# Projections of queries, keys and values with weight blocks of 512 columns, replaced in place chunk by chunk

## The chip, the cores and the metric

The kernel runs on one core of one Trainium2 chip. The metric is device time in microseconds (us) of one execution. The names of the engines are those of the profile: PE is TensorE's matmul, PEld its weight load, DVE is VectorE, ACT is ScalarE, POOL is GpSimd, SP is SyncE, which here only issues DMAs. SBUF is the on-chip memory of 128 partitions, PSUM the accumulators of the matmuls (8 banks of 512 float32 columns).

## The reference, cut to what matters

Two layers work on x of 2048 tokens by 1024. Each normalises x, multiplies it by one input matrix of 1024 by 4096, runs two attentions on the parts of the product, gates them, multiplies by an output matrix of 1024 by 1024 and adds the result to x.

```
for layer in range(DEPTH):                               # DEPTH = 2
    h = _rmsnorm(x, norm_g[layer])
    proj = jnp.einsum('bsd,dc->bsc', h, w_in[layer])     # 1024 -> 4096 columns
    qa, ka, va, ga, qd, kd, vd, gd = jnp.split(proj, cuts, axis=-1)   # 4 x 256, then 4 x 768
    oa = _stick_breaking(qa, ka, va) * silu(ga)
    qd = _partial_rope(_rmsnorm(heads(qd, 12), q_norm_g[layer]), pos)
    kd = _partial_rope(_rmsnorm(heads(kd, 12), k_norm_g[layer]), pos)
    od = _dilated_mixture(qd, kd, heads(vd, 12)) * silu(gd)
    x = x + concatenate([oa, od]) @ w_out[layer]
```

The change concerns the line `proj`, and of its 4096 columns those of qa, ka, va, qd, kd and vd (3072). The columns of ga and gd are the gates.

## The kernel before, in words

A layer has five stages: projection, stick-breaking attention (`_stick`), dilated attention (`_dilated`), output (`_output`), and then the next layer's projection. The class `Project` holds the first. Every float32 operand of a matmul is split into a high part that fp32r can hold and a low rest, and each product is three matmuls: high by high, high by low, low by high.

**The stationary and the moving operand.** `prep` (line 238) normalises 128 tokens, transposes them on PE (line 258) and stores their high and low parts, called hT. For queries, keys and values, `token_mm` (line 286) takes a 128 by 128 piece of hT as the stationary operand and 256 columns of weights as the moving one: 8 chunks k of the 1024 inputs, three matmuls each (lines 289 to 291), so 24 matmuls for 128 tokens. For the gates it is the other way round (lines 315 to 317): 128 columns of weights are stationary and 512 tokens of hT move. The output stage (lines 876, 879, 880) moves 512 columns of w_out past 128 stationary tokens.

**The weight blocks.** The loop over `cols` (line 299) goes through 16 blocks of 256 columns: three called sb (qa, ka, va), six called qk (128 columns of qd and 128 of kd each), three called v, four called g. `load_w` (line 200) loads the next block while this one is used: two DMAs or four into the raw pages H6 and H7, an ACT copy that makes the high part (line 212), and a subtraction for the low one (line 213), on POOL, except for the very first block, where it is on DVE. Blocks alternate between the pages F12, F13 and F2, F3.

**What follows a block's matmuls.** One group is 512 tokens in two PSUM banks (of four: 5, 0, 1, 2). For sb and v, DVE and ACT copy the banks to the pages S0 and S1 (lines 337 and 335), and SP stores them, for v three times in three orders (lines 346, 347, 350). For qk, ACT squares (line 356), DVE sums (line 357), POOL takes the power -0.5 (lines 135, 138), DVE scales (line 361), POOL applies gain and rotary (lines 368, 376 to 379), ACT and DVE split (lines 384, 385), PE transposes (line 393, 16 per group), DVE and ACT evict (lines 398, 396) and SP stores 512 KB at a time (line 399).

**What sets the order.** The kernel states instructions and tiles; a scheduler with a cost model of its own then fixes the order in which they stand on each engine, and places the waits. A page (F12, H6, S0, ...) is one buffer: a new tile on it waits until the last reader of the old one is done. Each engine works through its list in order, and so does SP with its DMAs.

Of the kernel before, what the change touches and what calls it, by code (L numbers as in the profile page):

```python
# [10 lines left out]
F32 = mybir.dt.float32  # L11
# [9 lines left out]
NT = 16  # L21
# [167 lines left out]
class Project:  # L189
# [10 lines left out]
    def load_w(self, parts, first=False):  # L200
# [3 lines left out]
        wh = mem.get(a, [128, NK, 256], F32R)  # L204
        wl = mem.get(b, [128, NK, 256], F32R)
# [9 lines left out]
        return wh, wl  # L215

# [5 lines left out]
    def begin(self):  # L222
# [10 lines left out]
        self.wblk = self.load_w([(0, QA, 256)], self.layer == 0)  # L233

    def hT(self, q, s, k):
        return self.hq[q][2 * s + k // 4][:, k % 4]
# [28 lines left out]
    def run(self, sb_scr, v_scr, qk_scr, g_scr, inject):  # L265
# [12 lines left out]
        r1 = xa[:, 512:768].rearrange("p (a b c) -> p a b c", a=4, c=16)  # L278
        r2 = xa[:, 768:1024].rearrange("p (a b c) -> p a b c", a=4, c=16)
# [6 lines left out]
        def token_mm(ps, wh, wl, c):  # L286
            q, cs = c // 4, slice(128 * (c % 4), 128 * (c % 4) + 128)
            for k in range(NK):
                nc.tensor.matmul(ps, hT(q, 0, k)[:, cs], wh[:, k], start=k == 0, stop=False)  # L289
                nc.tensor.matmul(ps, hT(q, 0, k)[:, cs], wl[:, k], start=False, stop=False)  # L290
                nc.tensor.matmul(ps, hT(q, 1, k)[:, cs], wh[:, k], start=False, stop=k == NK - 1)  # L291

        nxt = self.wblk
        cols = [("sb", 0, [(0, QA, 256)]), ("sb", 1, [(0, KA, 256)]), ("sb", 2, [(0, VA, 256)])]
        cols += [("qk", p, [(0, QD + 128 * p, 128), (128, KD + 128 * p, 128)]) for p in range(NPAIR)]
        cols += [("v", i, [(0, VD + 256 * i, 256)]) for i in range(3)]
        cols += [("g", 0, [(0, GA, 256)])]
        cols += [("g", 2 + 2 * i, [(0, GD + 256 * i, 256)]) for i in range(3)]
        for bi, (kind, idx, parts) in enumerate(cols):
            wh, wl = nxt  # L300
            if bi + 1 < len(cols):
                nxt = self.load_w(cols[bi + 1][2])
            if kind == "g":
                order = [(ct, tq) for ct in range(2) for tq in (2, 0, 3, 1)]
                if bi == len(cols) - 1:
                    order = [(ct, tq) for tq in (2, 0, 3, 1) for ct in range(2)]
                for gi, (ct, tq) in enumerate(order):
                    if bi == len(cols) - 1:
                        for f in inject.get(gi, ()):
                            f()  # L310
                    t = slice(512 * tq, 512 * tq + 512)
                    w = slice(128 * ct, 128 * ct + 128)
                    ps = pm.get([128, 512])
                    for k in range(NK):
                        nc.tensor.matmul(ps, wh[:, k, w], hT(tq, 0, k), start=k == 0, stop=False)  # L315
                        nc.tensor.matmul(ps, wh[:, k, w], hT(tq, 1, k), start=False, stop=False)  # L316
                        nc.tensor.matmul(ps, wl[:, k, w], hT(tq, 0, k), start=False, stop=k == NK - 1)  # L317
                    g = stg.get([128, 512])
                    nc.scalar.activation(g, ps, AF.Sigmoid)
                    nc.vector.tensor_tensor(out=g, in0=ps, in1=g, op=ALU.mult)  # L320
                    nc.sync.dma_start(out=g_scr[idx + ct, :, t], in_=g)
                continue
            for c4 in range(NT // 4):
                pss = []
                for c2 in range(2):
                    ps = pm.get([128, 2, 256])
                    for j in range(2):
                        token_mm(ps[:, j], wh, wl, 4 * c4 + 2 * c2 + j)
                    pss.append(ps)
                if kind in ("sb", "v"):  # L330
                    for c2, ps in enumerate(pss):
                        c = 4 * c4 + 2 * c2
                        st = stg.get([128, 2, 256])
                        if c2:
                            nc.scalar.copy(st, ps)
                        else:
                            nc.vector.tensor_copy(st, ps)  # L337
                        if kind == "sb":
                            nc.sync.dma_start(
                                out=sb_scr[idx].rearrange("(a c) d -> a c d", c=NT)[:, c:c + 2],  # L340
                                in_=st)
                            continue
                        for j in range(2):
                            src = st[:, j]
                            r, cc = (c + j) // 4, (c + j) % 4
                            nc.sync.dma_start(out=v_scr[idx, 0, 128 * (c + j):128 * (c + j) + 128], in_=src)
                            nc.sync.dma_start(
# [7 lines left out]
                for c2, ps in enumerate(pss):  # L355
                    nc.scalar.activation(qn[:, 2 * c2:2 * c2 + 2].rearrange("p a b c -> p a (b c)"), ps, AF.Square)
# [569 lines left out]
```

## Time and profile before

| | |
|---|---|
| median of 3 runs | 3266.57 us (3261.29 to 3266.58) |
| the profiled execution | 3269.15 us, of which the span from first to last instruction is 3267.4 us |
| PE busy | 3177.5 us, 97% of the span |
| DVE, ACT, POOL busy | 49%, 47%, 40% |
| first projection (0 to 602 us, without the gates) | PE busy 591.2 of 602 us |
| second projection (1640 to 2235 us, without the gates) | PE busy 594.3 of 595 us |
| granted TensorE clock, mean | 0.992 of full speed |

The projection without the gates takes about 1190 us of the 3267. A matmul's record lasts longer than its turn, since matmuls overlap: the time that one costs in a stream is the distance from one start to the next, which is called the pitch below. A few records of matmuls are missing from the trace, so pitches are taken between two events with a known number of matmuls between them.

### The profile page before, as it was taken

To read this page: it belongs to the slowest core of one execution; us is meant where nothing else is said; L and a number is where in the kernel's file an instruction comes from. 1 tells how busy PE (TensorE), PEld (TensorE's weight loads), DVE (VectorE), ACT (ScalarE), POOL (GpSimd) and SP (SyncE) were. 2 spreads that over 40 slices of the span, in tenths; PEclk is the share of its full clock that TensorE was granted. 3 is DMA by queue.
4 is the path that set the end of the run, shared out by engine and by line. 5 is a ranking of instruction groups with operands and counts; after the bars stand their busy time and mean duration, and the time that the engine had idled before them with its cause. 6 is when DMAs were issued, how large, how long until landed. Compare 5 with 4: busy or idle time off the path is not lost.

```text
span 3267.4 us, 66732 instructions
## 1 busy us (share of the span) xinstructions
PE 3177.5 (97%) x25808; PEld 2880.8 (88%) x25808; DVE 1605.1 (49%) x4067; ACT 1521.4 (47%) x4277; POOL 1317.2 (40%) x1342
## 2 busy tenths in 40 slices
PE   8999999999999999989999999999999999999899
PEld 8999999987777999877899999998877779988787
DVE  5034430014988777775140334301159887767721
ACT  5023221114777999962031232201147789988510
POOL 3067771012664344451021677611026744444500
PEclk9999999999999999999999999999999999999999
DMA  5222236416123556454441222363170235563443
GB/s 188 70 81 106 103 121 181 122 62 193 28 82 92 152 160 183 126 162 144 131 134 66 85 104 104 131 182 111 52 203 14 82 98 159 165 183 113 135 146 107
DMA packets 306429, 396.86 MB, mean 121 GB/s; under 512 B 16832, under 2 KB 225728, under 8 KB 295872
## 3 DMA queue, kind: packets, MB, share of 16 engines
q1 hardware_dynamic: 306112, 392.59, 39.2%
q8 instruction: 204, 3.34, 0.4%
q14 instruction: 113, 0.93, 0.1%
HBM read 235.24 MB, written 148.90 MB: 118 GB/s over the span
## 4 chain that ended last, share of the span: by engine, by line
PE 82%; DVE 5%; ACT 4%; POOL 4%; issue 3%; DMA 2%; SPq 0%; POOLq 0%; DVEq 0%; ACTq 0%
PE b L290 11%; PE b L291 11%; PE b L289 11%; PE b L676 7%; PE b L711 5%; PE b L697 5%; PE b L315 4%; PE b L317 4%; PE b L316 4%; PE b L879 3%; PE b L880 3%; PE b L876 3%; PE b L528 2%; PE b L393 2%; DVE G L495 2%
## 5 line engine op out<-in xcount | busy, mean ns | idle before, releaser
L291 PE MATMUL b<-F,F 128*128 128x256 f32 x2304 | 651.8, 283 | 0.0
L682 ACT ACTIVATE H<-H,T 128x256 f32<-128x256 f32 (+1 forms) x1152 | 522.7, 457 | 46.0 <-DVE T L678 43.7
L678 DVE CUSTOM_DVE_ANT_0 H<-b,M 128x256 f32<-128x256 f32 (+1 forms) x1152 | 368.2, 360 | 168.8 <-PE b L676 62.7
L291 PEld LDWEIGHTS b<-F,F 128*128 128x128 f32 x2304 | 440.4, 191 | 0.0
L290 PE MATMUL b<-F,F 128*128 128x256 f32 x1536 | 436.3, 284 | 0.0
L289 PE MATMUL b<-F,F 128*128 128x256 f32 x1536 | 434.9, 283 | 0.0
L290 PE MATMUL b<-F,G 128*128 128x256 f32 x1536 | 434.0, 283 | 0.0
L289 PE MATMUL b<-F,G 128*128 128x256 f32 x1536 | 433.5, 282 | 0.0
L501 POOL TENSOR_TENSOR G<-G,G 128x512 f32<-128x512 f32 (+3 forms) x320 | 320.3, 1015 | 228.9 <-DVE G L495 176.4
L676 PE MATMUL b<-F,F 128*128 128x256 f32 x2304 | 412.0, 303 | 0.3
L213 POOL TENSOR_TENSOR F<-H,F 128x1024 fp32r<-128x1024 f32 x62 | 154.2, 2500 | 605.3 <-ACT F L212 570.1
L495 DVE TENSOR_TENSOR_SCAN G<-G,b 128x513 f32<-128x513 f32 (+3 forms) x320 | 336.0, 1083 | 33.4 <-ACT G L494 33.1
L676 PEld LDWEIGHTS b<-F,F 128*128 128x128 f32 x2304 | 326.3, 190 | 20.1 <-issue 19.5
L697 PE MATMUL b<-ident,H 128*128 128x128 f32 x1800 | 293.0, 274 | 11.0 <-ACT H L699 5.5
L289 PEld LDWEIGHTS b<-F,F 128*128 128x128 f32 x1536 | 294.7, 192 | 0.0
L290 PEld LDWEIGHTS b<-F,F 128*128 128x128 f32 x1536 | 294.7, 192 | 0.0
L289 PEld LDWEIGHTS b<-F,G 128*128 128x128 f32 x1536 | 294.6, 192 | 0.0
L290 PEld LDWEIGHTS b<-F,G 128*128 128x128 f32 x1536 | 291.6, 190 | 0.0
L711 PE MATMUL b<-H,H 128*64 128x128 f32 x3600 | 229.5, 277 | 0.8 <-DVE H L699 0.8
L697 PEld LDWEIGHTS b<-ident,H 128*128 128x128 f32 x1800 | 215.5, 141 | 16.1 <-ACT H L699 8.5
L493 ACT ACTIVATE G<-b 128x512 f32<-128x512 f32 (+3 forms) x320 | 180.4, 566 | 103.5 <-PE b L486 88.3
L337 DVE COPY S<-b 128x512 f32<-128x512 f32 x48 | 33.2, 691 | 390.5 <-PE b L291 347.9
(161 smaller groups left out, 6849.0 us busy)
## 6 DMA issues: line engine op xcount, KB each, us to landing
qk_l<-H SPq DMA_DIRECT2D x96, 512.0 KB
F<-qk_l SPq DMA_DIRECT2D x48, 1024.0 KB
v_l<-S SPq DMA_DIRECT2D x288, 128.0 KB
H<-v_l SPq DMA_DIRECT2D x72, 512.0 KB
F<-qk_l SPq DMA_DIRECT2D x48, 512.0 KB
H<-in_w_in SPq DMA_DIRECT2D x40, 512.0 KB
g_l<-S SPq DMA_DIRECT2D x64, 256.0 KB
G<-mixa_l SPq DMA_DIRECT2D x32, 448.0 KB
```

What stands on the lines that cost most here:

```text
L213: (nc.vector if first else nc.gpsimd).tensor_tensor(out=wl[:, ks], in0=raw, in1=wh[:, ks].bitcast(F32), op=ALU.subtract)
L289: nc.tensor.matmul(ps, hT(q, 0, k)[:, cs], wh[:, k], start=k == 0, stop=False)
L290: nc.tensor.matmul(ps, hT(q, 0, k)[:, cs], wl[:, k], start=False, stop=False)
L291: nc.tensor.matmul(ps, hT(q, 1, k)[:, cs], wh[:, k], start=False, stop=k == NK - 1)
L493: nc.scalar.activation(g[:, 512 - n:512], z[:, :n], AF.Sigmoid, scale=-0.125)
L495: nc.vector.tensor_tensor_scan(out=r[:, 0:n + 1][:, ::-1], data0=g[:, 512 - n:513][:, ::-1], data1=z[:, 0:1].to_broadcast([128, n + 1]), i ...
L501: nc.gpsimd.tensor_tensor(out=b[:, :n], in0=b[:, :n], in1=r[:, 1:n + 1], op=ALU.mult)
L676: pin(nc.tensor.matmul(sc[:, h], qb, kv, start=s == 0, stop=s == 1))
L678: nc.vector.tensor_tensor_reduce(out=pe[:, h, :un], in0=sc[:, h, u0:u0 + un], in1=mk[:, m0:m0 + un], scale=-0.125, scalar=3.0e38, op0=ALU. ...
L682: nc.scalar.activation(pe[:, h, :un], pe[:, h, :un], AF.Exp, scale=-1.0, bias=st[:, 0, p, h, b:b + 1], accum_out=st[:, 1, p, h, b:b + 1])
L697: pin(nc.tensor.transpose(tp[:, ch, h], pe[:, h, 128 * w:128 * w + 128], ident))
L711: pin(nc.tensor.matmul(ob[64 * h:64 * h + 64, b % 4], vq[(pr * 3 + p) * 2 + (b - ch) // 8][:, (b - ch) % 8, 64 * h:64 * h + 64], ts[:, ch, h],
```

## The change: what it does

Of the twelve blocks of queries, keys and values, ten become five of 512 columns (called wide): qa with ka, three of 256 columns of qd and 256 of kd, and the first 512 of vd. The columns of va and the last 256 of vd stay blocks of 256 (narrow), va now first. The gates are as before. A wide block fills all four pages: chunks 0 to 3 of k in F2 (high) and F3 (low), chunks 4 to 7 in F12 and F13. There is no second set, so the next block's chunk is written over the old one as soon as the last group of tokens has used it. To this end the first and the last group of a block run with k as the outer loop, over two PSUM banks; the groups between run token by token. A group is now 256 tokens by 512 columns. Each chunk has a DMA of its own or two (`wide_raw`), an ACT copy and a subtraction on DVE (`wide_split`). The qk groups are stored 256 KB at a time, and the sb and v stores are as large as each row block of 256 columns.

```
     def load_w(self, parts, first=False):
-        wh = mem.get(a, [128, NK, 256], F32R)
-        wl = mem.get(b, [128, NK, 256], F32R)
+        wh, wl = (self.wt[p].rearrange("p (k f) -> p k f", k=NK) for p in (a, b))
...
+    def wide(self, k):
+        a, b = ("F2", "F3") if k < 4 else ("F12", "F13")
+        cs = slice(512 * (k % 4), 512 * (k % 4) + 512)
+        return self.wt[a][:, cs], self.wt[b][:, cs]
+
+    def wide_raw(self, parts, k):
+        if k % 2 == 0:
+            self.rawp = mem.get(f"H{6 + k // 2 % 2}", [128, 2, 512])
+        raw = self.raws[k] = self.rawp[:, k % 2]
+        for dst, col, n in parts:
+            nc.sync.dma_start(out=raw[:, dst:dst + n], in_=self.w_l[:, k, col:col + n])
+
+    def wide_split(self, k):
+        wh, wl = self.wide(k)
+        raw = self.raws.pop(k)
+        nc.scalar.copy(wh, raw)
+        nc.vector.tensor_tensor(out=wl, in0=raw, in1=wh.bitcast(F32), op=ALU.subtract)
...
-        self.wblk = self.load_w([(0, QA, 256)], self.layer == 0)
+        self.wt = {p: mem.get(p, [128, 2048], F32R) for p in ("F12", "F13")}
+        self.wblk = self.load_w([(0, VA, 256)], self.layer == 0)
...
+        def mm3(ps, c, k, wh, wl):
+            q, cs = c // 4, slice(128 * (c % 4), 128 * (c % 4) + 128)
+            nc.tensor.matmul(ps, hT(q, 0, k)[:, cs], wh, start=k == 0, stop=False)
+            nc.tensor.matmul(ps, hT(q, 0, k)[:, cs], wl, start=False, stop=False)
+            nc.tensor.matmul(ps, hT(q, 1, k)[:, cs], wh, start=False, stop=k == NK - 1)
...
+        for k in range(4):
+            self.wide_raw(wide[0][2], k)
+            self.wide_split(k)
+        narrow("sb", 2, *self.wblk, True)        # va; then raw and split of chunks 4 to 7
+        for bi, (kind, idx, parts) in enumerate(wide):
+            nxt = wide[bi + 1][2] if bi + 1 < len(wide) else None
+            for g in range(NT // 2):
+                pss = [pm.get([128, 512]) for _ in range(2)]
+                edge = g in (0, NT // 2 - 1)
+                if g == NT // 2 - 1 and nxt:
+                    for k in range(4):
+                        self.wide_raw(nxt, k)
+                for k in range(NK) if edge else (None,):
+                    for j in range(2):
+                        for kk in range(NK) if k is None else (k,):
+                            mm3(pss[j], 2 * g + j, kk, *self.wide(kk))
+                    if g == NT // 2 - 1:
+                        if nxt:
+                            self.wide_split(k)
+                            if k < 4:
+                                self.wide_raw(nxt, k + 4)
+                        elif k == 3:
+                            self.wn = 1
+                            self.wblk = self.load_w(tail[0][2])
+                if kind == "qk":
+                    qk_out(idx, pss, 2 * g)
...
+        for bi, (kind, idx, parts) in enumerate(tail):   # the last of vd, then the gates
```

On PE, before: in layer 0 the second group of the qk blocks' first one (names: output bank, then moving weights, then stationary hT), 256 columns at a time and one token block after the other.

```order
L289 MATMUL b2_201_2369<-F2_140_1439,F10_75_492 128x256
L290 MATMUL b2_201_2369<-F3_141_1440,F10_75_492 128x256
L291 MATMUL b2_201_2369<-F2_140_1439,F5_77_494 128x256
L289 MATMUL b2_201_2369<-F2_140_1439,F10_75_492 128x256
L290 MATMUL b2_201_2369<-F3_141_1440,F10_75_492 128x256
```

On PE, now: the end of the first wide qk block in layer 0 (last chunk in F12 and F13, banks 1 and 2) and the first matmul of the second one (F2, bank 5).

```order
L310 MATMUL b1_242_2248<-F13_5_213,F11_76_493 128x512
L311 MATMUL b1_242_2248<-F12_4_212,F6_78_495 128x512
L309 MATMUL b2_243_2249<-F12_4_212,F11_76_493 128x512
L310 MATMUL b2_243_2249<-F13_5_213,F11_76_493 128x512
L311 MATMUL b2_243_2249<-F12_4_212,F6_78_495 128x512
L309 MATMUL b1_242_2248<-F12_4_212,F11_76_493 128x512
L310 MATMUL b1_242_2248<-F13_5_213,F11_76_493 128x512
L311 MATMUL b1_242_2248<-F12_4_212,F6_78_495 128x512
L309 MATMUL b2_243_2249<-F12_4_212,F11_76_493 128x512
L310 MATMUL b2_243_2249<-F13_5_213,F11_76_493 128x512
L311 MATMUL b2_243_2249<-F12_4_212,F6_78_495 128x512
L309 MATMUL b5_258_2385<-F2_100_587,G1_8_222 128x512
```

A matmul now moves 512 columns, the two banks of an edge group alternate after each three matmuls, and the new block starts in the pages that the old one used first.

On POOL, before: the split of a weight block (line 213) among the qk work of layer 0.

```order
L379 TENSOR_TENSOR H2_190_2271<-X_99_585 128x16x16
L213 TENSOR_TENSOR F3_213_2468<-H6_214_2469,F2_212_2467 128x1024
L135 TENSOR_SCALAR U3_203_2419<-U3_203_2419 128x16
L213 TENSOR_TENSOR F3_213_2468<-H7_215_2474,F2_212_2467 128x1024
L138 TENSOR_TENSOR U3_203_2419<-U3_203_2419,half_67 128x16
```

On DVE, now: the splits (line 234) at the same handover as above, among the qk work of groups 5, 6 and 7 (lines 334, 338, 358, 369).

```order
L234 TENSOR_TENSOR F3_101_588<-H6_244_2250,F2_100_587 128x512 x2
L234 TENSOR_TENSOR F3_101_588<-H7_245_2255,F2_100_587 128x512
L338 TENSOR_TENSOR H2_232_2197<-b5_230_2147,U2_233_2198 128x512
L338 TENSOR_TENSOR H2_232_2197<-b0_231_2148,U2_233_2198 128x512
L234 TENSOR_TENSOR F3_101_588<-H7_245_2255,F2_100_587 128x512
L369 COPY H0_224_2117<-b3_225_2118 128x512
L234 TENSOR_TENSOR F13_5_213<-H6_246_2268,F12_4_212 128x512
L369 COPY H1_227_2132<-b6_228_2133 128x512
L234 TENSOR_TENSOR F13_5_213<-H6_246_2268,F12_4_212 128x512
L234 TENSOR_TENSOR F13_5_213<-H7_247_2289,F12_4_212 128x512
L334 TENSOR_REDUCE U3_249_2335<-H3_248_2334 128x16
L358 TENSOR_TENSOR H4_234_2212<-H2_232_2197,H4_234_2212 128x8x64
```

The subtractions have left POOL's list and stand in DVE's, half as long and twice as many, between the steps of the last groups.

On SP, now: the loads of the next block's chunks at the same handover (line 227: H6 for chunks 4 and 5, H7 for 6 and 7) and the qk stores (line 371).

```order
L371 DMA qk_l0_202<-H1_215_2031 128x2x256 x2
L227 DMA H6_246_2268<-in_w_in 128x256 x4
L227 DMA H7_247_2289<-in_w_in 128x256 x2
L371 DMA qk_l0_202<-H0_224_2117 128x2x256 x2
L371 DMA qk_l0_202<-H1_227_2132 128x2x256 x2
L227 DMA H7_247_2289<-in_w_in 128x256 x2
L227 DMA H6_344_3094<-in_w_in 128x256 x4
```

The last chunk's two loads stand behind four stores of a qk group; the raw loads for the block after next follow at once.

## Rows read from the trace of the kernel before

**Rows 1.** The page, busy time of each engine (share of the span), instructions.
```profile
PE 3177.5 (97%) x25808; PEld 2880.8 (88%) x25808; DVE 1605.1 (49%) x4067; ACT 1521.4 (47%) x4277; POOL 1317.2 (40%) x1342
```

**Rows 2.** Windows: stretch, length, busy us (instructions), granted clock, DMA share, GB/s.
```profile
190.00:480.00 290.00, 290.00 (x2535) 290.00 (x2534) 117.60 (x159) 87.02 (x146) 218.36 (x190) 1.00 0.29 102
484.00:602.00 118.00, 118.00 (x994) 118.00 (x993) 9.71 (x14) 11.97 (x18) 13.17 (x11) 1.00 0.61 178
1640.00:2235.00 595.00, 594.30 (x5091) 593.93 (x5091) 170.11 (x227) 138.64 (x233) 269.17 (x238) 1.00 0.35 116
```

**Rows 3.** The page, chain that ended last: share of the span by line.
```profile
PE b L290 11%; PE b L291 11%; PE b L289 11%; PE b L676 7%; PE b L711 5%; PE b L697 5%; PE b L315 4%; PE b L317 4%; PE b L316 4%; PE b L879 3%; PE b L880 3%; PE b L876 3%; PE b L528 2%; PE b L393 2%; DVE G L495 2%
```

**Rows 4.** Timeline, DVE in the v blocks: start, duration, line, [idle before].
```profile
524.30 0.69 DVE L337 COPY S<-b 128x512 f32<-128x512 f32 x1 [10.48 <-PE b L291]
...
570.16 0.69 DVE L337 COPY S<-b 128x512 f32<-128x512 f32 x1 [10.72 <-PE b L291]
```

**Rows 5.** Timeline, DVE in the gate blocks.
```profile
632.95 0.69 DVE L320 TENSOR_TENSOR S<-b,S 128x512 f32<-128x512 f32 x1 [4.75 <-ACT S L319]
638.39 0.69 DVE L320 TENSOR_TENSOR S<-b,S 128x512 f32<-128x512 f32 x1 [4.75 <-ACT S L319]
643.94 0.69 DVE L320 TENSOR_TENSOR S<-b,S 128x512 f32<-128x512 f32 x1 [4.86 <-ACT S L319]
...
676.78 0.69 DVE L320 TENSOR_TENSOR S<-b,S 128x512 f32<-128x512 f32 x1 [4.75 <-ACT S L319]
```

**Rows 6.** Timeline, DVE in the output stage of layer 0.
```profile
1534.21 0.69 DVE L900 TENSOR_TENSOR G<-b,G 128x512 f32<-128x512 f32 x1 [3.90 <-PE b L880]
...
1623.70 0.69 DVE L900 TENSOR_TENSOR G<-b,G 128x512 f32<-128x512 f32 x1 [3.90 <-PE b L880]
```

**Rows 7.** Groups of instructions, 190 to 480 us: busy us, mean ns, idle before.
```profile
L385 DVE TENSOR_TENSOR H<-H,H 128x512 fp32r<-128x512 f32 x46 | 34.8, 796 | 23.1 <-ACT H L384 23.1
L384 ACT CAST H<-H 128x512 fp32r<-128x512 f32 x44 | 25.1, 619 | 20.3 <-POOL H L379 20.3
L212 ACT CAST F<-H 128x1024 fp32r<-128x1024 f32 x12 | 11.9, 1046 | 0.0
L213 POOL TENSOR_TENSOR F<-H,F 128x1024 fp32r<-128x1024 f32 x12 | 31.0, 2585 | 10.4 <-ACT F L212 9.9
```

**Rows 8.** Two lines' instructions: count, duration ns min/median/max, first and last start.
```profile
L385 DVE TENSOR_TENSOR H<-H,H x96: 677/684/1550, 189.3 to 2113.0; 128x512 fp32r<-128x512 f32 x96
L213 DVE TENSOR_TENSOR F<-H,F x2: 1214/1220/1225, 10.5 to 12.2; 128x1024 fp32r<-128x1024 f32 x2
```

**Rows 9.** Timeline, 160 to 215 us, the first qk group: ACT, DVE, POOL.
```profile
176.05 0.60 ACT L356 ACTIVATE H<-b 128x512 f32<-128x512 f32 x1 [5.06 <-PE b L291]
181.21 1.29 DVE L361 TENSOR_TENSOR H<-b,U 128x512 f32<-128x512 f32 x2 [3.32 <-POOL U L138]
186.92 0.74 POOL L379 TENSOR_TENSOR H<-X 128x256 f32<-128x256 f32 x1
189.33 1.28 DVE L385 TENSOR_TENSOR H<-H,H 128x512 fp32r<-128x512 f32 x2
```

**Rows 10.** The chain in order of time: start, length, what.
```profile
2.17 7.19 DMA H<-in_w_in
11.71 10.02 DMA H<-in_w_in
192.69 1.31 PE b L393 x16
```

**Rows 11.** Windows at the start of layer 0, columns as in group 2.
```profile
20.00:30.00 10.00, 9.66 (x82) 9.40 (x80) 5.59 (x8) 7.53 (x13) 7.61 (x7) 1.00 0.80 271
30.00:40.00 10.00, 8.63 (x73) 8.46 (x74) 7.99 (x11) 5.61 (x11) 2.51 (x6) 1.00 0.82 264
```

**Rows 12.** Timeline, SP in the v blocks: three stores of one page.
```profile
530.61 0.33 SPq L346 DMA_DIRECT2D v_l<-S  x1
530.99 0.53 SPq L347 DMA_DIRECT2D v_l<-S  x1
531.57 0.56 SPq L350 DMA_DIRECT2D v_l<-S  x1
```

**Rows 13.** Waits, 484 to 602 us: who waited for whom, us, times, longest.
```profile
DVE S L337 <- DMA v_l<-S: 21.8, 2, 11.1
ACT S L335 <- DMA v_l<-S: 29.7, 3, 10.7
```

More of the change, by code (lines that the diff above doesn't have):

```diff
@@ L284, in run @@
         ssr = mem.ring("U2", "U3")
-        def token_mm(ps, wh, wl, c):
+        def mm3(ps, c, k, wh, wl):
             q, cs = c // 4, slice(128 * (c % 4), 128 * (c % 4) + 128)
[L288 to L291, printed above, removed]
@@ new lines, in mm3, with v_out @@
+            nc.tensor.matmul(ps, hT(q, 0, k)[:, cs], wh, start=k == 0, stop=False)
+            nc.tensor.matmul(ps, hT(q, 0, k)[:, cs], wl, start=False, stop=False)
+            nc.tensor.matmul(ps, hT(q, 1, k)[:, cs], wh, start=False, stop=k == NK - 1)
+        def v_out(i, n, src, c):
+            r, cc = c // 4, c % 4
+            for j in range(n):
+                sv = src[:, 256 * j:256 * j + 256]
+                nc.sync.dma_start(out=v_scr[i + j, 0, 128 * c:128 * c + 128], in_=sv)
+                nc.sync.dma_start(
+                    out=v_scr[i + j, 1, 512 * cc:512 * cc + 512].rearrange(
+                        "(n r a) d -> r n a d", n=4, r=4)[r], in_=sv)
+                nc.sync.dma_start(
+                    out=v_scr[i + j, 2].rearrange("(j c a) d -> c j a d", c=NT, a=8)[c], in_=sv)
@@ new lines, in run, with narrow @@
+        self.wt.update({p: mem.get(p, [128, 2048], F32R) for p in ("F2", "F3")})
+        wide = [("sb", 0, [(0, QA, 512)])]
+        wide += [("qk", i, [(0, QD + 256 * i, 256), (256, KD + 256 * i, 256)]) for i in range(3)]
+        wide += [("v", 0, [(0, VD, 512)])]
+        tail = [("v", 2, [(0, VD + 512, 256)]), ("g", 0, [(0, GA, 256)])]
+        tail += [("g", 2 + 2 * i, [(0, GD + 256 * i, 256)]) for i in range(3)]
+        def narrow(kind, idx, wh, wl, roll):
+            for g in range(NT // 2):
+                ps = pm.get([128, 2, 256])
+                for j in range(2):
+                    for k in range(NK):
+                        mm3(ps[:, j], 2 * g + j, k, wh[:, k], wl[:, k])
+                if roll and g == NT // 2 - 1:
+                    for k in range(4, NK):
+                        wide_next(k)
+                st = stg.get([128, 512])
+                (nc.scalar.copy if g % 2 else nc.vector.tensor_copy)(st, ps.rearrange("p a b -> p (a b)"))
+                for j in range(2):
+                    (sb_out if kind == "sb" else v_out)(idx, 1, st[:, 256 * j:256 * j + 256], 2 * g + j)
```

192 lines of the change are left out of this document (85 added, 107 removed).

## The prediction

> **What bounds the kernel now.** I read the page first: PE is busy 97% of the span, no other engine half of it [rows 1]. A share of busy time does not say what a shorter matmul is worth, so next come the windows of the stages that the change touches: in the qk blocks of layer 0 PE is busy 290.00 of 290 us, in the v blocks 118.00 of 118, in the second layer's whole projection 594.30 of 595, all at a granted clock of 1.00, that is 2.4 GHz [rows 2]. The chain of waits says the same: the three token matmuls (lines 289 to 291) are 33% of the span's last chain, the largest share of any stage, and what follows them in the qk blocks does not appear [rows 3]. So in this stage a microsecond less on PE is a microsecond less in all, as long as the other engines keep up.
>
> What does a matmul cost? Its record lasts 283 ns or so, but the next one starts long before it ends. I take two evictions with a known number of matmuls between them. For 256 columns: DVE copies of line 337 at 524.30 and 570.16 us, four groups of 96 matmuls apart: 45.86 / 384 = 119.4 ns [rows 4]. For 512 columns there are two kinds of stream. In the gates, 632.95 to 676.78 us holds eight groups of 24: 43.83 / 192 = 228.3 ns; single groups there differ (5.44 us, so 226.7 ns, and 5.55 us, so 231.3) [rows 5]. In the output stage, 1534.21 to 1623.70 us holds sixteen groups of 24: 89.49 / 384 = 233.0 ns [rows 6]. Twice the columns cost 1.91 to 1.95 times the pitch: about 10 ns of each matmul do not depend on the columns.
>
> **The change part by part: the matmuls.** Five wide blocks of 16 token tiles with 24 matmuls each are 1920 matmuls of 512 columns a layer, 3840 in both, in place of 7680 of 256. At the gates' pitch a pair saves 2 x 119.4 - 228.3 = 10.5 ns, in all 40.3 us. At the gates' best group it is 12.1 ns, 46.5 us; at the output stage's pitch 5.8 ns, 22.3 us. Which one holds the trace cannot show, since no stream before has hT stationary and 512 weights moving: the output stage has that assignment (tokens stationary, weights moving), the gates have this stage's pages. I take the gates' mean, which lies between the ends and is drawn from the same pages F and G. The transposes (16 in 1.31 us, one batch a group [rows 10]) are as many as before, 384 a layer.
>
> **The qk work.** A qk group is now 256 tokens by 512 columns instead of 512 by 256, with the same number of elements in every step, so ACT, DVE and POOL do the same per group; the group lasts 48 x 0.2283 + 1.31 = 12.27 us instead of 96 x 0.1194 + 1.31 = 12.77. POOL, the fullest of them with 218.36 of 290 us, gives away the splits (31.0 us of that [rows 2, 7]), so it has more room than before. Latency: in the first qk group the second square starts at 176.05 us and DVE's split, which the transposes wait for, ends at 190.61, 14.6 us later [rows 9]. In the new order the transposes of a group stand 79 matmuls after its last one, 18.0 us and a batch of transposes: 3 to 5 us to spare. An edge group finishes both banks together, which costs one square more, 0.60 us. The scaled banks are free at 182.5, 6.5 us after the square, and the bank is wanted again after a whole group. Hidden: 0 us.
>
> **The splits.** 80 subtractions of 512 columns move from POOL to DVE. The two that DVE did before took 1.22 us for 1024 [rows 8], so 0.61 each; with the ACT copy, half of 1.046 [rows 7], a chunk is ready some 1.3 us after its release with the handshakes. DVE gets 49 us more over both layers, in stages where it is busy 117.60 of 290 us or less [rows 2]. That is cover, but not everywhere: at the start of layer 0 four splits (2.4 us) come between the normalisations, where DVE is busy 13.6 of 20 us and PE already idles 1.7 [rows 11]. I charge half, 1.2 us, and 0.3 in layer 1; the bounds are 0 and 5 us.
>
> The line that does the same kind of subtraction, 385, mostly takes 684 ns, but up to 1550 and 796 on average [rows 7, 8], with POOL at work beside it. The Trainium skill, page "SBUF — State Buffer", section "Who interferes with whom", says that a VectorE instruction with two SBUF inputs and a GpSimd instruction that reads SBUF exclude each other, the second waiting the first out. The spread of line 385 agrees. It speaks against moving the splits to DVE while POOL works on the qk blocks; what it would make of the time is the third rival.
>
> **The handovers.** A chunk is free after its six matmuls in the last group, 1.37 us apart, and wanted again one group later, so 10.9 us (12.27 - 1.37) after its release. Chunks 0 to 3 have their raw columns in H6 and H7 beforehand: 1.3 us, hidden. Chunks 4 and 5 must first be loaded, after chunk 1 is split (2 x 1.37 + 1.3 = 4.0 us into the group). The two weight loads in the chain of waits, of 512 KB in the crowded start, took 7.19 and 10.02 us [rows 10]; a chunk pair here is 512 KB too. With 10.02 chunk 5 is ready at 16, wanted at 19. Chunk 7's load stands behind four stores of a qk group, whose transposes and evictions end near 10 us: ready at 10.5 + 10.0 + 1.3 = 22, wanted at 23. So even with the worst landing it just fits; SP needs 0.33 to 0.56 us for an issue [rows 12], small change. Two handovers a layer are between narrow and wide: from va, the first missing chunk is wanted 5.5 us after its release; into the last v block, POOL's two subtractions (2.585 us each [rows 7]) end 11.7 us into the group, and are wanted near 12.6. Charge: 0.1 us for each of 12, bounds 0 and 0.5.
>
> **The v stores.** Evictions there already wait now and then for the stores of the page before [rows 13]. A page has six stores, some 3.4 us of issues [rows 12], and comes round every 10.96 us now, 11.46 before. PE has four banks to run ahead with, so I cost this at nothing; without that cover it would give back what the v block gains, 0.5 us for each of 16 groups, 8 us.
>
> **Sum.** -40.3 + 1.5 + 1.2 = -37.6 us. Against the profiled execution, 3269.15 us (a span of 3267.4 and 1.75 around it), that is 3231.6; the profiled one lies 2.6 us over the median of the runs, 3266.57, so the time to expect is 3229.
>
> **Rivals.**
> *The output stage's pitch (14%).* For it: the same assignment of operands, and 233.0 ns held through 384 matmuls. Against it: its stationary tiles lie in other pages (H), and 256 columns run here at a fixed part no larger than in the gates. Gain 22.3 - 2.7 = 19.6: 3247.
> *Handovers exposed, slower (5%).* Place: chunks 4 to 7 of each new block. If a load waits on SP behind stores that wait for evictions, and the splits behind it on ACT and DVE, PE stops in the first group with nothing else to do, since no other weights are in SBUF. The break-even is 40.3 / 12 = 3.4 us a handover. Ten us more on the load of the last chunks than assumed, a second landing of 10.02, would make chunk 7 late by 9 us less 1.3 of slack, some 7.7 us: 12 x 7.7 = 92, so 3266.6 - 40.3 + 92 = 3318. Against it: the landings assumed are already those of the crowded start (DMA share 0.80 and more [rows 11]; 0.29 in the qk blocks [rows 2]).
> *DVE late at the handovers, still faster (7%).* If each of 8 splits and 4 subtractions of line 385 at a qk handover waits 0.87 us for POOL (1550 - 684 [rows 8]), DVE has 10 us more to do in two groups, 26.5 us in 24.5: 2 us late, on six handovers 12 us: 3241.
> *No gain (4%).* The pitch goes with the columns (238.8 ns): then the time is 3266.6 + 2.7 = 3269. Both streams of 512 columns in the trace speak against it. The Trainium skill, page "TensorE: Matmul & The Clock Gate", section "Back-to-back issue gap", gives columns / 2.4 plus 2.5 ns; an estimate by that page is a gain of 3840 x 2.5 = 9.6 us. The trace does not agree: 119.4 and 228.3 ns lie 12.7 and 15.0 above columns / 2.4.
>
> **How the numbers follow.** 70% for the forecast, and 14, 7, 5 and 4 for the rivals. The forecast's own range: the best pitch and no losses, 3266.6 - 46.5 = 3220, less 4 for a pitch under 226.7 (hT may do a little better than any gate group); upwards the pitch 231.3 of the slower gate group (28.8 us) with 6 us of losses, 3244. To leave out no more than 2 in 10 it must take in the second rival's 3247 with a few us of losses: 3216 to 3250, which leaves out the slow rival, no gain and part of the losses. This kernel's measurement can tell some 0.2%, 6.5 us, from no change. Faster by more than that: 70 + 14 + 7 = 91%; the same: 4%; slower: 5%.
>
> **What would show it.** In the changed profile: token matmuls with 512 columns, 1920 a layer, PE busy to the last tenth from 12 us to the gates, and a stage shorter by some 20 us a layer; evictions of the wide blocks 5.4 to 5.6 us apart in sb and v. A wait of PE on ACT or DVE of line 233 or 234 in the first group of a block would show the handovers exposed; evictions 5.7 us apart would show no gain; line 234 at 1.5 us, the collision with POOL. The prediction is wrong if PE idles more than 10 us in the two projections, or if the pitch lies outside 224 to 234 ns.

## The result and the profile after

The changed kernel takes 3226.73 us (median of 4 runs, 3222.49 to 3228.57), the kernel before, run beside it, 3265.88 us. The ratio is 0.9879, 95% interval 0.9865 to 0.9892: 39 us or 1.2% faster. In a later comparison on one chip the unaltered changed kernel came out at 0.9873 (0.9858 to 0.9888).

The page of the changed kernel: busy time of each engine, then the chain that ended last by line.

```profile
PE 3137.9 (97%) x21968; PEld 2683.2 (83%) x21968; DVE 1648.3 (51%) x4147; ACT 1534.4 (48%) x4317; POOL 1234.4 (38%) x1302
...
PE b L310 11%; PE b L311 11%; PE b L309 11%; PE b L732 7%; PE b L767 5%; PE b L753 5%; PE b L451 4%; PE b L453 4%; PE b L452 4%; PE b L935 4%; PE b L936 4%; PE b L932 3%; PE b L584 3%; PE b L367 2%; ACT H L738 2%
```

PE has 3840 matmuls fewer and is busy 39.6 us less than in [rows 1]; its share of the span is the same 97%, and the token matmuls (now lines 309 to 311) still lead the chain, as in [rows 3]. So the stage is bound by what bound it before, only by less of it. Where the time went is seen when the span of the profiled execution is cut at the first gate matmul and the last output matmul of each layer:

| stretch | before, us | after, us | difference |
|---|---|---|---|
| start to the first gate matmul, layer 0 | 610.2 | 590.1 | -20.1 |
| gates, attentions, output of layer 0 | 1029.9 | 1029.1 | -0.8 |
| projection without the gates, layer 1 | 594.7 | 575.5 | -19.2 |
| the rest | 1032.6 | 1032.1 | -0.5 |

Of the 40.6 us between the two spans 39.3 lie in the two projections. The other 1.3 lie in stretches that the change does not touch; the last of these took 1032.1 us here and 1027.9 in a later profile of the same kernel (run 5), so a few us there say nothing. The windows in the projections, columns as in [rows 2]: the start, the qk blocks of layer 0, part of the v block, and most of layer 1's projection.

```profile
20.00:30.00 10.00, 9.42 (x74) 8.50 (x73) 8.39 (x13) 9.37 (x19) 2.64 (x6) 1.00 0.81 272
30.00:40.00 10.00, 10.00 (x88) 10.00 (x87) 8.08 (x11) 5.21 (x10) 2.23 (x6) 1.00 0.78 266
...
180.00:460.00 280.00, 280.00 (x1447) 234.74 (x1446) 130.71 (x181) 90.73 (x159) 200.32 (x183) 1.00 0.32 106
480.00:540.00 60.00, 60.00 (x267) 49.66 (x266) 3.46 (x5) 4.94 (x7) 2.44 (x1) 1.00 0.60 174
1640.00:2190.00 550.00, 550.00 (x2965) 470.85 (x2963) 178.37 (x247) 132.43 (x229) 225.39 (x209) 1.00 0.36 114
```

PE is busy without a gap in the windows from 30 us on, and the granted clock is 1.00. At the start it does better than in [rows 11]: 19.42 of 20 us instead of 18.29.

The pitch, read as in [rows 4 to 6]. DVE evicts every second group of 24 matmuls in the wide sb block:

```profile
89.36 0.69 DVE L430 COPY S<-b 128x512 f32<-128x512 f32 x1 [5.61 <-PE b L311]
100.42 0.69 DVE L430 COPY S<-b 128x512 f32<-128x512 f32 x1 [10.37 <-PE b L311]
111.30 0.69 DVE L430 COPY S<-b 128x512 f32<-128x512 f32 x1 [10.19 <-PE b L311]
...
143.94 0.69 DVE L430 COPY S<-b 128x512 f32<-128x512 f32 x1 [10.19 <-PE b L311]
```

From 100.42 to 143.94 us are 192 matmuls: 226.7 ns each. The first distance, 11.06 us, still contains 24 matmuls of tokens 384 to 511 and is longer. PE's own rows at the start of the second qk block show the other pitch (start, duration, line):

```profile
255.69 0.39 PE L310 MATMUL b<-F,F 128*128 128x512 f32 x1
255.91 0.39 PE L311 MATMUL b<-F,F 128*128 128x512 f32 x1
256.14 0.40 PE L309 MATMUL b<-F,G 128*128 128x512 f32 x1
256.38 0.39 PE L310 MATMUL b<-F,G 128*128 128x512 f32 x1
256.61 0.40 PE L311 MATMUL b<-F,G 128*128 128x512 f32 x1
...
262.44 0.40 PE L309 MATMUL b<-F,G 128*128 128x512 f32 x1
...
263.38 1.48 PE L367 MATMUL b<-ident_r,H 128*128 128x128 f32 x16
...
265.93 0.40 PE L309 MATMUL b<-F,G 128*128 128x512 f32 x1
...
267.33 0.40 PE L309 MATMUL b<-F,G 128*128 128x512 f32 x1
```

The stationary operand is the name behind the comma: with tokens 0 to 255 (page G1; this is an edge group) 27 matmuls take from 256.14 to 262.44 us, 233.3 ns each. Over the whole trace three quarters of the wide matmuls (tokens 512 to 2047) run at 226.7 to 226.8 ns and one quarter (tokens 0 to 511) at 233.1 in the mean, all together at 228.4.

The handover just before that block: ACT copies of the last two chunks (line 233), DVE splits (line 234), SP's loads.

```profile
248.38 4.84 SPq L227 DMA_DIRECT2D H<-in_w_in  x6
253.32 2.20 SPq L371 DMA_DIRECT2D qk_l<-H  x4
255.57 6.52 SPq L227 DMA_DIRECT2D H<-in_w_in  x8
...
255.17 0.62 ACT L233 CAST F<-H 128x512 fp32r<-128x512 f32 x1 [0.93 <-DMA H<-in_w_in]
...
259.92 0.62 ACT L233 CAST F<-H 128x512 fp32r<-128x512 f32 x1 [0.81 <-DMA H<-in_w_in]
...
260.57 0.69 DVE L234 TENSOR_TENSOR F<-H,F 128x512 fp32r<-128x512 f32 x1 [0.63 <-ACT F L233]
```

Chunk 7's load stands behind four stores, as the order said; it is issued at 255.57, landed by 259.92 (4.35 us at most), and is split by 261.26. The new block starts at 256.14 and reaches chunk 7 at 267.33: 6.1 us to spare, the smallest margin of this handover.

### The profile page after: what moved, and what is told of

Read it like the earlier page. It is cut to its first block, busy times and chain, and to the rows that moved or that the text cites. A ratio compares the mean times of both kernels' runs of the same rounds, so it can differ in the third digit from the quotient of the medians.

```text
span 3226.8 us, 59494 instructions
## 1 busy us (share of the span) xinstructions
PE 3137.9 (97%) x21968; PEld 2683.2 (83%) x21968; DVE 1648.3 (51%) x4147; ACT 1534.4 (48%) x4317; POOL 1234.4 (38%) x1302
## 4 chain that ended last, share of the span: by engine, by line
PE 81%; DVE 5%; ACT 4%; POOL 4%; issue 3%; DMA 2%; SPq 0%; POOLq 0%; ACTq 0%; DVEq 0%
PE b L310 11%; PE b L311 11%; PE b L309 11%; PE b L732 7%; PE b L767 5%; PE b L753 5%; PE b L451 4%; PE b L453 4%; PE b L452 4%; PE b L935 4%; PE b L936 4%; PE b L932 3%; PE b L584 3%; PE b L367 2%; ACT H L738 2%
## 5 line engine op out<-in xcount | busy, mean ns | idle before, releaser
L311 PE MATMUL b<-F,F 128*128 128x512 f32 (+1 forms) x1344 | 484.1, 360 | 0.4 <-DVE F L282 0.3
L732 PE MATMUL b<-F,F 128*128 128x256 f32 x2304 | 412.3, 303 | 0.3 <-DVE T L734 0.3
L732 PEld LDWEIGHTS b<-F,F 128*128 128x128 f32 x2304 | 326.4, 190 | 20.1 <-issue 19.5
L310 PE MATMUL b<-F,G 128*128 128x512 f32 (+1 forms) x896 | 324.7, 362 | 0.0
L309 PE MATMUL b<-F,G 128*128 128x512 f32 (+1 forms) x896 | 324.3, 362 | 0.0
L310 PE MATMUL b<-F,F 128*128 128x512 f32 (+1 forms) x896 | 323.2, 361 | 0.0
L309 PE MATMUL b<-F,F 128*128 128x512 f32 (+1 forms) x896 | 321.9, 359 | 0.0
L311 PEld LDWEIGHTS b<-F,F 128*128 128x128 f32 x1344 | 253.7, 189 | 38.4 <-DVE F L282 0.8
L135 POOL TENSOR_SCALAR U<-U 128x16 f32<-128x16 f32 (+1 forms) x80 | 33.7, 421 | 536.1 <-DVE U L334 315.5
L738 ACT ACTIVATION_READ_ACCUMULATOR H<-H,T 128x1 f32 x1152 | 219.3, 190 | 0.0
L767 PEld LDWEIGHTS b<-H,H 128*64 128x64 f32 x3600 | 193.8, 137 | 25.9 <-issue 23.4
L212 POOL TENSOR_TENSOR F<-H,F 128x1024 fp32r<-128x1024 f32 x22 | 53.9, 2456 | 380.7 <-ACT F L211 164.0
L333 ACT ACTIVATE H<-b 128x512 f32<-128x512 f32 x96 | 57.5, 600 | 294.8 <-PE b L311 293.8
L309 PEld LDWEIGHTS b<-F,G 128*128 128x128 f32 x896 | 168.9, 189 | 26.6
```

The source lines that it names most:

```text
L309: nc.tensor.matmul(ps, hT(q, 0, k)[:, cs], wh, start=k == 0, stop=False)
L310: nc.tensor.matmul(ps, hT(q, 0, k)[:, cs], wl, start=False, stop=False)
L311: nc.tensor.matmul(ps, hT(q, 1, k)[:, cs], wh, start=False, stop=k == NK - 1)
L732: pin(nc.tensor.matmul(sc[:, h], qb, kv, start=s == 0, stop=s == 1))
L738: nc.scalar.activation(pe[:, h, :un], pe[:, h, :un], AF.Exp, scale=-1.0, bias=st[:, 0, p, h, b:b + 1], accum_out=st[:, 1, p, h, b:b + 1])
L767: pin(nc.tensor.matmul(ob[64 * h:64 * h + 64, b % 4], vq[(pr * 3 + p) * 2 + (b - ch) // 8][:, (b - ch) % 8, 64 * h:64 * h + 64], ts[:, ch, h],
```

## The experiments

Ratios are to the kernel before on the same chip (its medians: 3269.11 in the first four, 3266.69 in the next four, 3268.23 in the last four); the changed kernel stands at 0.9873 to 0.9879.

**1. Halves: the gain without the wide matmul.**

```
+   for f in range(2):
+       fs = slice(256 * f, 256 * f + 256)
-       mm3(pss[j], 2 * g + j, kk, *self.wide(kk))
+       mm3(pss[j][:, fs], 2 * g + j, kk, *(w[:, fs] for w in self.wide(kk)), f)
```

> The changed kernel with every matmul of 512 columns done as two of 256 (first half of the bank, then the second, for each chunk); blocks, loads, splits, handovers and groups stay. Theory (the gain is the pitch of the matmuls): the 7680 matmuls cost about 119.4 to 120 ns each again, so the time goes back by 3840 x 10.4 to 11.6 = 40 to 45 us, to 3267 to 3271. Rival (a part of the gain comes from elsewhere, from the splits moved to DVE, the order of the groups or the stores): the time rises by clearly less than 36 us, say to 3245.

Measured 3267.69 us, ratio 0.9995 (0.9987 to 1.0004). Its evictions in the sb block (another kernel, the same stage as line 430 above):

```profile
100.68 0.69 DVE L432 COPY S<-b 128x512 f32<-128x512 f32 x1 [10.72 <-PE b L311]
112.20 0.69 DVE L432 COPY S<-b 128x512 f32<-128x512 f32 x1 [10.83 <-PE b L311]
```

11.52 us for 96 matmuls is 120 ns, and the whole gain is gone. Blocks, handovers, groups and the place of the splits are those of the changed kernel. So all of them together bring or take at most some 4 us against the kernel before (the interval): the gain is the pitch. One of them could still make up for another.

**2. The splits back on POOL.**

```
-   nc.vector.tensor_tensor(out=wl, in0=raw, in1=wh.bitcast(F32), op=ALU.subtract)
+   nc.gpsimd.tensor_tensor(out=wl, in0=raw, in1=wh.bitcast(F32), op=ALU.subtract)
```

> The changed kernel with its 80 subtractions of 512 columns on POOL. Theory (no handover is on the path, whichever engine splits): POOL does one in 1.3 us as before, the chunk is ready 0.6 us later plus POOL's queue; the slack in the changed kernel's trace is 4 us and more, so the time stays within 5 us of the changed kernel, 3222 to 3232. Rival 1 (the move to DVE was needed: POOL's splits queue behind the power of line 138, 3 us, and the rotary, and the last chunks come late): 6 handovers of qk blocks late by 2 to 5 us each, 12 to 30 us slower, 3239 to 3257. Rival 2 (the splits on DVE collide with POOL and cost time on the path): faster by over 3 us.

Measured 3236.74 us, 0.9901 (0.9887 to 0.9915): by the ratios 7 to 9 us slower than the changed kernel. The theory's 3222 to 3232 fell, and so did rival 2, which wanted it faster. But rival 1 is not it either: the chunks are not late. PE's wait in 180 to 620 us (us, times, longest):

```profile
PE b L309 <- DVE H L338: 2.3, 2, 1.3
```

The timeline of POOL and DVE at the second qk handover in the same kernel:

```profile
259.32 1.30 POOL L234 TENSOR_TENSOR F<-H,F 128x512 fp32r<-128x512 f32 x1
...
260.99 1.31 POOL L234 TENSOR_TENSOR F<-H,F 128x512 fp32r<-128x512 f32 x1
...
262.95 3.01 POOL L234 TENSOR_TENSOR F<-H,F 128x512 fp32r<-128x512 f32 x2
265.93 3.35 POOL L138 TENSOR_TENSOR U<-U,half 128x16 f32<-128x16 f32 x1
...
269.32 1.29 DVE L338 TENSOR_TENSOR H<-b,U 128x512 f32<-128x512 f32 x2 [0.67 <-POOL U L138]
```

The subtractions stand ahead of the power (line 138), which starts at 265.93 us; DVE's scaling (line 338) waits for it, and only this frees the two banks that PE wants next. In the changed kernel the same scaling starts at 261.51. PE stops for 1.0 to 1.3 us there, twice in each layer; its idle time in the two projections is 4.6 us. Against the changed kernel's profile the projections are 5.5 us longer; where the rest of the 7 to 9 us lies was not traced.

**3. The edge order in all groups.** The slower pitch at the start of each block could come from the edge order.

```
-   edge = g in (0, NT // 2 - 1)
+   edge = True
+   cc = (g, g + 8) if kind == "v" else (2 * g, 2 * g + 1)
...
-   mm3(pss[j], 2 * g + j, kk, *self.wide(kk))
+   mm3(pss[j], cc[j], kk, *self.wide(kk))
```

> The changed kernel with the edge order (k outside, two banks in turn after three matmuls each) in all groups of the wide blocks, 2880 matmuls more of the 3840. In the v block, a group's two banks belong to token blocks g and g + 8, not 2g and 2g + 1. The changed kernel's trace shows 226.7 ns in the groups that run token by token and about 233 in the edge groups. Theory A (alternating the banks costs it): 233 ns everywhere, 2880 x 6.6 = 19 us slower, 3246. Theory B (the two stationary pieces 512 bytes apart in one page cost it): 233 ns in sb and qk, 226.7 in the v block, whose pieces lie in different pages: 15 us slower, 3242. Rival (what runs beside the handover costs it, loads and splits): the pitch stays at 226.7 outside the first and the last group, no change, 3227.

Measured 3225.84 us, 0.9872 (0.9855 to 0.9890): no change. In sb both banks now finish together, and two of DVE's evictions read

```profile
105.37 0.69 DVE L431 COPY S<-b 128x512 f32<-128x512 f32 x1 [10.23 <-PE b L311]
116.25 0.69 DVE L431 COPY S<-b 128x512 f32<-128x512 f32 x1 [10.19 <-PE b L311]
```

again 10.88 us for 48. Alternating the banks costs nothing, so both theories fell. The trace showed what the slow stretch follows: in the v block, where tokens 0 to 511 were now spread over the first four groups, each beside tokens 1024 to 1535, it lasted four groups (mean 231.7 ns) instead of two. So the rival's reason, the work beside the handover, fell too. The slow stretch goes with the tokens whose hT is in G1.

**4. One block for all.** The weights of the first wide block serve for all five; the other 32 chunks of a layer are neither loaded nor split.

```
-   if g == NT // 2 - 1 and nxt:
-       for k in range(4):
-           self.wide_raw(nxt, k)
...
-   if nxt:
-       self.wide_split(k)
-       if k < 4:
-           self.wide_raw(nxt, k + 4)
```

> The changed kernel without any replacement of wide blocks: the weights of the first wide block (qa, ka) are used for the other four as well, and their 32 chunks a layer are not loaded and not split (that part of the computation is left out); groups and edge order stay. Theory (the handovers are hidden): the same time within 2 us, 3224 to 3229, and only if the loads or splits disturb the pitch of the edge groups up to 6 us less. Rival (handovers cost on the path): faster by 12 times what one costs; 0.5 us each would give 3221, 1 us each 3215.

Measured 3227.56 us, 0.9873 (0.9859 to 0.9886): the time of the changed kernel. Replacing the weights in place costs nothing that can be measured; less than some 4 us would not show in the time.

**5. The changed kernel again.**

> The changed kernel itself, unaltered, so that the three kernels beside it are compared on the same chip: 3222 to 3231 us, and the ratio to the kernel before 0.9865 to 0.9892 again.

Measured 3224.79 us, 0.9873 (0.9858 to 0.9888).

**6. Other addresses.**

```
-   sizes = [(f"F{i}", 2048) for i in range(14)] + [("G0", 6156), ("G1", 6156)]
-   sizes += [(f"H{i}", 1024) for i in range(8)] + ...
+   sizes = [(f"H{i}", 1024) for i in (2, 3, 4, 5)] + [("G1", 6156)]
+   sizes += [(f"F{i}", 2048) for i in (0, 1, ..., 8, 10, 11, 12, 9, 13)] + [("G0", 6156)]
+   sizes += [(f"H{i}", 1024) for i in (0, 1, 6, 7)] + ...
```

> The changed kernel with the SBUF pages in another order of addresses, nothing else: H2 to H5 and G1 come first, then F0 to F8, F10 to F12, and F9, F13, G0 behind them, with H0, H1, H6, H7 and the small ones last. Before, G1 and H stood behind all F pages and G0. In the changed kernel's trace the slow pitch (233 ns against 226.7) is that of tokens 0 to 511, whose hT lies in G1, and of the output stage, whose stationary tiles lie in H2 to H5. Theory A (where the stationary piece lies decides): tokens 0 to 511 go to 226.7, tokens 1024 to 1535 (G0, F9) to 233, the output stage to 226.7: 1536 x 6.3 = 9.7 us faster, 3217. Theory B (any operand in the far pages costs it): besides, every matmul on the low half of chunks 4 to 7 (F13) is slow, a sixth of the 3840, 4 us back: 3221. Rival (position: the first groups of a block or stage are slow whatever their pages): no change, 3227.

Measured 3210.70 us, 0.9831 (0.9817 to 0.9846): 14 us faster than the changed kernel, the best of all. DVE's evictions in its output stage (line 957) and, below, the same ones of the changed kernel (line 956):

```profile
1533.40 0.69 DVE L957 TENSOR_TENSOR G<-b,G 128x512 f32<-128x512 f32 x1 [4.75 <-PE b L937]
1538.84 0.69 DVE L957 TENSOR_TENSOR G<-b,G 128x512 f32<-128x512 f32 x1 [3.75 <-PE b L937]
```

```profile
1530.13 0.69 DVE L956 TENSOR_TENSOR G<-b,G 128x512 f32<-128x512 f32 x1 [4.90 <-PE b L936]
1535.72 0.69 DVE L956 TENSOR_TENSOR G<-b,G 128x512 f32<-128x512 f32 x1 [3.90 <-PE b L936]
```

5.44 against 5.59 us for 24 matmuls: this part of the output stage went from 233 to 226.7 ns. Over the whole trace its mean pitch went from 233.0 to 227.1, which for its 1536 matmuls is 9.1 us. Tokens 0 to 511 went to 226.7 as well, in the gates too; tokens 1024 to 1535, whose hT is in the page now put far out, stayed there. The ten wide blocks are 4.4 us shorter together. In both traces every engine has the same instructions in the same order, and the edit moves pages only. So it is the addresses, not the position in the block; but neither theory is whole, since it is not simply a far page either. Three runs on this follow (9 to 11).

**7. All blocks wide.** The narrow blocks of va and of the last of vd become one more wide block.

```
-   self.wblk = self.load_w([(0, VA, 256)], self.layer == 0)
+   for k in range(4, NK):
+       self.wide_raw([(0, QA, 512)], k)
+       self.wide_split(k)
...
+   wide += [("vb", 2, [(0, VA, 256), (256, VD + 512, 256)]), ("v", 0, [(0, VD, 512)])]
```

> The changed kernel with the two narrow blocks of a layer (va, and the last 256 columns of vd) joined to one more wide block; the first block is then the wide one of qa and ka, whose chunks 4 to 7 are loaded first, and the last wide block is vd's first 512, in whose last group chunks 4 to 7 go first. Theory (the gain is 2 x 120 - 228 ns for each pair of matmuls wherever PE is full): 384 pairs a layer x 11.7 ns = 4.5 us, 9 us in both, 3218. Rival (the start pays for it: PE waits in layer 0 for 2 MB of weights and for the normalisation beside them): 5 to 15 us given back, 3222 to 3235.

Measured 3221.82 us, 0.9863 (0.9848 to 0.9877): 3 us under the changed kernel, with intervals that overlap. By the times alone it is inconclusive: neither 9 us nor a loss. The profiled executions say more: cut as in the table above, the two projections are 6.6 us shorter than in run 5's (8.6 than in the first profile of the changed kernel), most of the 9 us expected, and the stretches that this edit does not touch are 4.5 us longer than in run 5's.

**8. One raw page: the handover's cover taken away.**

```
-   self.rawp = mem.get(f"H{6 + k // 2 % 2}", [128, 2, 512])
+   self.rawp = mem.get("H6", [128, 2, 512])
```

> The changed kernel with one raw page (H6) for all chunks of the wide blocks in place of two (H6, H7): only two chunks can be loaded ahead, and each following pair waits for the split of the pair before. In the changed kernel a chunk is ready at least some 4 us before it is wanted. Theory (hidden by that slack, and exposed once it is used up): a pair takes a landing of 2.5 to 4.5 us and two splits of some 2 us, so the last pair is ready 18 to 23 us after the first release and wanted at 18 to 20: 0 to 3 us late at each of 8 handovers, 0 to 24 us slower, 3227 to 3251, with PE waiting for line 234 or 233 in the first group of the blocks. Rival (PE's order of work gives no room at all, every later chunk is paid in full): 5 us a handover and more, over 3267.

Measured 3227.42 us, 0.9883 (0.9863 to 0.9904): not told apart from the changed kernel. The last two splits of the second qk handover did come later, to 266.7 us instead of 261.26, and yet PE never waited, so the theory of an exposed handover fell. Its DVE at that place, its window over the qk and v blocks of layer 0, and PE's rows meanwhile:

```profile
263.79 2.93 DVE L234 TENSOR_TENSOR F<-H,F 128x512 fp32r<-128x512 f32 x2 [0.26 <-ACT F L233]
```

```profile
180.00:600.00 420.00, 420.00 (x2263) 358.32 (x2262) 148.80 (x202) 109.21 (x185) 219.19 (x198) 1.00 0.42 131
```

```profile
264.57 0.39 PE L311 MATMUL b<-F,F 128*128 128x512 f32 x1
...
265.27 0.40 PE L311 MATMUL b<-F,G 128*128 128x512 f32 x1
...
268.54 0.40 PE L311 MATMUL b<-F,F 128*128 128x512 f32 x1
```

For these tokens line 311 reads F from chunk 4 on and G before. So in that group the order that the scheduler has put on PE goes on to the next token block's chunks 0 to 3 before it comes back for 6 and 7, which the changed kernel's does not.

**9 to 11. Where an operand starts.** Counted from the sizes of the tiles, in the changed kernel the pages F and G0 start 96 bytes past a multiple of 128 in each partition, G1 and H 32 past; in run 6 all operands of these stages started at 96. Three kernels keep the old order of the pages and make all starts alike: at 96, at 32, at 0.

```
-   ... ("G0", 6156), ...          ar = mem.get("G0", [128, 6156])
+   ... ("G0", 6176), ...          ar = mem.get("G0", [128, 6176])
-   neg1 = const.tile([128, 1], ...)
+   neg1 = const.tile([128, 24], ...)      # second run: 64 bytes up; third: [128, 16], 32 bytes up
```

> The changed kernel with one number altered: the page G0 is 6176 columns long instead of 6156, so that G1, H0 to H7 and all behind them move up by 64 bytes in every partition; the order of the pages is the old one. In the changed kernel F0 to F13 and G0 start 96 bytes past a multiple of 128, G1 and H0 to H7 start 32 bytes past one; with other addresses (the run with the pages reordered, 14 us faster) all operands of the projections and the output started at 96. Theory A (a mismatch of 64 bytes between the operands of a matmul, or a bad start of one of them, makes the pitch 233): now all start at 96, the pitch is 227 everywhere, 3211 +- 3. Theory B (which pages are far from each other in SBUF decides): the far pages stay far, no change, 3225 +- 3.

> As the run with G0 of 6176 columns, and all pages 64 bytes further up, so that all operands of the projections and the output start 32 bytes past a multiple of 128. Theory A1 (only a mismatch between stationary and moving costs): 227 ns everywhere, 3211 +- 3. Theory A2 (the stationary operand at 32 is what is slow, wherever the moving one lies): all 3840 + 1536 + the gates' 1536 matmuls go to 233 ns, 45 us slower than A1, 3256, and the narrow blocks a little more. Theory B: no change against the changed kernel, 3225.

> As the run with G0 of 6176 columns, and all pages 32 bytes further up, so that they start at multiples of 128. Theory A1 (mismatch alone): as that run, 3211 +- 3. Rival (32 bytes off a multiple of 64 also costs): the pitch falls below 226.7 ns, each ns is worth 6.9 us over the 6912 matmuls of 512 columns, so under 3205.

Measured 3225.72 (0.9877, 0.9859 to 0.9894), 3224.29 (0.9868, 0.9852 to 0.9883) and 3224.95 us (0.9871, 0.9857 to 0.9884): no change, all three. The mean pitch of the output stage goes from 233.0 to 231.8 or 231.9 ns, that of tokens 0 to 511 from 233.1 to 232.9. The starts are worth about 1 ns in the one and 0.2 in the other, not 6; the theory of run 6's start bytes fell, and what is left is which pages lie where.

**12. All wide, with G0 longer.** Runs 7 and 9 in one.

> The run in which all blocks are wide, with G0 of 6176 columns. If both gains are of PE's pitch, in different matmuls or the same, they add up: the 3 us of the wide blocks (3224.8 to 3221.8, not clear of noise) and the 14 us of the addresses, 3207 to 3209. If the narrow blocks were what the addresses helped, less: 3211.

Measured 3219.16 us, 0.9852 (0.9838 to 0.9867): against 0.9863 and 0.9877 of its parts nothing clear was added. In the profiled executions the two projections are 3.7 and 4.6 us shorter than in run 9's, close to the 9 us that run 7 expected of the wide blocks. All wide with the pages of run 6 was not run.

## Why the prediction was right, step by step

It said 3229 us (3216 to 3250); 3226.73 was measured. In the profiled executions the sum was -37.6 us, and the spans differ by 40.6.

- **The matmuls, -40.3 us.** Measured: 3840 x (238.8 - 228.4) = 39.9 us, and run 1 takes all of it back. That the gates' mean hit the pitch is in part luck. The prediction argued with the common pages F and G, and the slow group is the same in both: tokens 0 to 511 (G1). But it costs 231.3 ns in the gates [rows 5] and 233.1 in the wide blocks, and the gates have a third kind of group, on tokens 1536 to 2047, which the next row of the kernel before ends (with 643.94 in [rows 5], 5.48 us or 228.3 ns):

```profile
649.42 0.69 DVE L320 TENSOR_TENSOR S<-b,S 128x512 f32<-128x512 f32 x1 [4.79 <-ACT S L319]
```

  In the wide blocks those tokens run at 226.7. That the two means come out at 228.3 and 228.4 could not be read from the rows.
- **The first rival, the output stage's pitch.** Its premise, that the assignment of operands sets 233 ns, is refuted twice: three quarters of the wide matmuls have that assignment and run at 226.7, and run 6 changes addresses alone and brings the output stage there too. What spoke against it, "its stationary tiles lie in other pages (H)", pointed the right way; that H's place alone does it is not shown, since run 6 moved nearly all pages.
- **The losses, 2.7 us.** Nearly all of them were not there: the matmuls are worth 39.9 us and the projections got 39.3 shorter, which leaves 0.6. The start was charged 1.2 us in layer 0; PE was busy 1.2 us more in its first 40 (30.36 us after, 29.17 before). The handovers were charged 1.2; PE has no gap at any of them, and run 4 finds no cost within its 4 us. So this term was charged some 2 us too high. The difference between 3229 and 3226.7 itself lies within the scatter of the runs.
- **The margin of the handovers.** The prediction gave chunk 7 one microsecond with a landing of 10.02 us, from the crowded start; the landing is at most 4.35 and the margin 6.1. The slow rival's 7.7 us takes the slack off twice (10.02 less 1.3 is 8.7, which would have made it some 3331 instead of 3318). It also rested on "nothing else to do": run 8 refutes that, since the next token block's matmuls on loaded chunks fill the time.
- **The splits on DVE.** Counted as hidden, and hidden they are. Each takes 0.69 us and not 0.61. The collision with POOL is there; line 234 in the whole trace (count, shortest, median, longest in ns), its group in 180 to 460 us, and one such split with POOL beside it:

```profile
L234 DVE TENSOR_TENSOR F<-H,F x80: 676/692/1189, 21.1 to 2059.2; 128x512 fp32r<-128x512 f32 x80
```

```profile
L234 DVE TENSOR_TENSOR F<-H,F 128x512 fp32r<-128x512 f32 x24 | 19.1, 804 | 5.0 <-ACT F L233 4.8
```

```profile
251.35 3.32 POOL L343 TENSOR_TENSOR H<-H,T 128x512 f32<-128x512 f32 x2 [1.47 <-DVE H L338]
...
252.33 1.19 DVE L234 TENSOR_TENSOR F<-H,F 128x512 fp32r<-128x512 f32 x1
```

  All 12 splits that start while POOL is in a gain multiplication (line 343) take 0.94 to 1.19 us, the 8 that start in its rotary (lines 350 to 352) 0.69 to 0.96. The 23 that start within the power (line 138, 3 us long) take 0.68 to 0.71, as do the 37 that start beside no POOL instruction. So what a split costs depends on the POOL instruction that it meets. 24 x 0.11 us is 2.7 us of DVE, in blocks where it has 149 to spare; line 358, the former 385, no longer shows it (685 ns in the mean against 796 in [rows 7]). In the kernel before, the 12 of its 96 that took 1.55 us are just those that started within a split on POOL (line 213), and 82 of the others took 0.68 to 0.69. So the third rival took its 0.87 us from a collision with the very instructions that the change moves away from POOL; it left with them, and no split came to 1550 ns. What the prediction missed is the other side: that the splits left POOL is worth 7 to 9 us (run 2). In the kernel before they stood there too, but in larger pieces and without a wait for a handover, and PE did not wait.
- **The v stores.** The evictions wait longer than in [rows 13], and PE's four banks still cover it (60.00 of 60 us above). Waits of the line in 455 to 540 us (us, times, longest):

```profile
DVE S L430 <- DMA v_l<-S: 44.3, 5, 12.0
ACT S L430 <- DMA v_l<-S: 41.0, 4, 12.8
```

- **No gain.** The Trainium skill, page "TensorE: Matmul & The Clock Gate", section "Back-to-back issue gap", gives columns / 2.4 plus 2.5 ns for an isolated matmul at the higher clock; the estimate by it was a gain of 9.6 us. The traces decide against it for this stream: 120.0 and 226.7 ns lie 13.3 ns above columns / 2.4, both of them, and where the pitch is 226.7 that part is what a wider matmul saves.

## What to carry to other kernels

Where PE is full, take the cost of a matmul from the distance between two evictions with a known count between them, and look whether the groups of one stage differ: here one and the same shape ran at 226.7 to 233.1 ns, and a mean over groups of another stage was right only because two different mixes came out alike. Charge a wait only with the work that the scheduler can't put in its place. When an instruction moves off an engine, what it frees may be what stood behind it in that queue (here a power on POOL that frees PSUM banks), rather than its own time.

## What the runs showed that was not expected

The same matmul of 512 columns with the same operations beside it takes 226.7 or about 233 ns, and the addresses of the pages in SBUF decide which: tokens 0 to 511 and the output stage change with the order of the pages (run 6, 14 us in all). It is not the position in the block, not the turn of the banks (run 3), and the start within 128 bytes explains about 1 ns of the 6 in the output stage (runs 9 to 11). Which relation between the addresses decides stays open: counted from the sizes of the tiles, G0 lies 157 to 181 KB into a partition in run 6 and is fast, and G1 lay 140 to 165 KB in the changed kernel and was slow.
